# The low part of every weight: a negated copy on ScalarE and an accumulating DMA in place of a subtraction on VectorE

## The chip, the cores and the metric

One core of a Trainium2 chip runs the whole step. The metric is the device time of one execution in microseconds (us). Three timed runs of the kernel before took 2784.03, 2787.16 and 2788.79 us; the median is 2787.16 us.

## The reference

One denoising step of a small backbone with two layers, on 640 tokens of width 1024: 512 latent tokens and 128 context tokens. A layer is a half-step SwiGLU, a token mixer (layer 0: windowed attention; layer 1: a Hyena long convolution) and a second half-step SwiGLU. Each of the six sub-layers is modulated by a condition, gated and normalised.

```python
h = modulate(x, mod[:, 0], mod[:, 1])
f = swiglu(h, ffn_w1, ffn_w2)              # (silu(g) * u) @ w2, with [g, u] = h @ w1 and 2816 hidden columns
x = layer_norm(alpha * x + 0.5 * mod[:, 2] * f)
h = modulate(x, mod[:, 3], mod[:, 4])
out = attn(...)  or  hyena(...)            # projections w_qkv, w_o, or w_in, w_out
x = layer_norm(alpha * x + mod[:, 5] * out)
h = modulate(x, mod[:, 6], mod[:, 7])
x = layer_norm(alpha * x + 0.5 * mod[:, 8] * swiglu(h, ...))
mod = silu(cond) @ ada_w + ada_b           # 9 rows of 1024 a layer
```

All data are float32. The arithmetic is kept near float32 although TensorE multiplies rounded numbers (below).

## The kernel before

**Split operands.** TensorE runs on `float32r`, a rounded float32. So each operand `a` stands as a high part `ah = round(a)` and a low part `al = a - ah`, and a product takes three matmuls: `ah*bh + al*bh + ah*bl`. For weights these are the tiles `wh` and `wl`, for activations `hh`/`hl` (normalised input), `ah`/`al` (SwiGLU), `zh`/`zl` (Hyena).

**Weight units.** All weights come in 170 units in the order of use: tiles of 128 partitions by 2048 numbers (1 MiB), or by 1536 for three quarters of the second SwiGLU matrices (`w2a`, 0.75 MiB). `w_dma` (L108) loads a unit raw from memory into one of two buffers `wr`, by a DMA that SyncE issues. `w_split` (L118) makes the two parts: ScalarE copies `wr` to `wh` with rounding (L93), and VectorE subtracts, `wl = wr - wh` (L94). The subtraction runs on GpSimd in 11 units, which `run_steps` (L520) picks in the groups of three units (six steps), and three more units at the start and in attention are split by other engines (L128, L129). So 167 units go through `split`, the line that is changed. Units are counted from 0 here. After the split the raw buffer is free, and `w_split` asks for the next raw load (L135).

**Order.** Six `w` buffers hold three units. `w_get(u)` (L137) is called at the start of each step on unit u and, where fewer than three are live, splits one unit ahead. As a rule, unit u+2 is split when the first step on u begins, that is, when the matmuls on u-1 have given back their buffers. Engines take their instructions strictly in the order in which the code writes them. The text calls the time from the start of a unit's ScalarE copy to the first matmul that reads its `wl` the slack of the unit.

**Steps.** The 640 tokens run in two halves of 320 columns. A step takes one unit for one half: 48 matmuls of 320 columns. Most units are used for half 0 and at once for half 1; in groups of three units, at the ends of sub-layers, half 0 goes through all three units before half 1, so that the normalisation of half 0 (`ln_sched`, L328) runs beside half 1. It consists of a mean by matmul (`mu`), squares on ScalarE (`sq`), their sum on GpSimd (L351, L354), the reciprocal root on VectorE in small instructions (`rstd`, L470, with `ly` at L475), and a matmul that spreads it (`rs`, L366), for which the next use of `x` waits.

**Beside it.** `bg_step` (L233) computes the modulation in the background: GpSimd issues a 512 KB load `ar` (L231) two steps ahead, VectorE reduces it (L245). A load `ar` waits on GpSimd until VectorE has read the buffer's last contents. Its condition vector `cond` is loaded the same way (L222, 1 MiB).

Of the kernel before, what the change touches and what calls it, by code (L numbers as in the profile page):

```python
# [12 lines left out]
AF = mybir.ActivationFunctionType  # L13
ALU = mybir.AluOpType
# [28 lines left out]
class Kernel:  # L43
# [74 lines left out]
    def w_split(self, copy=None, sub=None):  # L118
        i = self.ws
        if i >= self.wlim:  # L120
            return
        self.w_dma(i + 1)
        shape = self.units[i][1]
        r = self.raw.pop(i)
        hi = self.wp.tile(shape, F32R, tag="w", name="wh")
        lo = self.wp.tile(shape, F32R, tag="w", name="wl")
        if copy is not None:
            copy.tensor_copy(out=hi, in_=r)  # L128
            sub.tensor_tensor(out=lo, in0=r, in1=hi.bitcast(F32), op=ALU.subtract)  # L129
        else:  # L130
            self.split(hi, lo, r, self.weng)
        self.wt[i] = (hi, lo)
        self.wlive.add(i)
        self.ws += 1
        self.w_dma(i + 3)  # L135
# [1631 lines left out]
```

## Time and profile before

| | |
|---|---|
| timed runs, median | 2787.16 us |
| the profiled execution's own time | 2792.72 us |
| its span, first to last instruction | 2791.0 us |
| TensorE (PE) busy | 2697.1 us, 97% |
| VectorE (DVE) busy | 1694.0 us, 61% |
| ScalarE (ACT) busy | 881.7 us, 32% |
| GpSimd (POOL) busy | 579.7 us, 21% |
| moved by DMA | 289.36 MB, mean 104 GB/s |

Busy times are unions of the instructions of an engine. Matmuls overlap each other (each shows some 0.31 us, and they start 0.147 us apart), so PE's busy time says where it had work, not how fast it ran. PEld is the weight load beside the matmuls. SP is SyncE. A DMA's landing is the time at which its data are reported as written.

### The profile page before, as it was taken

To read this page: it belongs to the slowest core of one execution; us is meant where nothing else is said; L and a number is where in the kernel's file an instruction comes from. 1 tells how busy PE (TensorE), PEld (TensorE's weight loads), DVE (VectorE), ACT (ScalarE), POOL (GpSimd) and SP (SyncE) were. 2 spreads that over 40 slices of the span, in tenths; PEclk is the share of its full clock that TensorE was granted. 3 is DMA by queue.
4 is the path that set the end of the run, shared out by engine and by line. 5 is a ranking of instruction groups with operands and counts; after the bars stand their busy time and mean duration, and the time that the engine had idled before them with its cause. 6 is when DMAs were issued, how large, how long until landed. Compare 5 with 4: busy or idle time off the path is not lost. (4 is left out here: it accounts for less than half of the span.)

```text
span 2791.0 us, 42388 instructions
## 1 busy us (share of the span) xinstructions
PE 2697.1 (97%) x17402; PEld 2528.2 (91%) x17402; DVE 1694.0 (61%) x3065; ACT 881.7 (32%) x1507; POOL 579.7 (21%) x639
## 2 busy tenths in 40 slices
PE   9989999998899999999999999999999899999997
PEld 3569999998854999999999999998998899999997
DVE  5865867748965577676766633337658855323334
ACT  3552222214576342222233122224332333122222
POOL 3541000005212520000041000005108842000002
PEclk8889999999899999999999999999999999999998
DMA  6243544421100235454512312221223321212121
GB/s 240 107 158 108 196 154 157 164 83 66 48 3 16 83 111 178 136 181 142 175 68 99 129 62 87 71 85 47 91 90 120 131 80 65 87 61 91 61 76 39
DMA packets 65018, 289.36 MB, mean 104 GB/s; under 512 B 8255, under 2 KB 13583, under 8 KB 46520
## 3 DMA queue, kind: packets, MB, share of 16 engines
q1 hardware_dynamic: 45736, 217.39, 22.4%
q0 software_dynamic: 18720, 69.21, 7.3%
q8 instruction: 137, 2.24, 0.3%
q14 instruction: 57, 0.47, 0.1%
q10 hardware_dynamic: 368, 0.04, 0.0%
HBM read 270.61 MB, written 16.01 MB: 103 GB/s over the span
## 5 line engine op out<-in xcount | busy, mean ns | idle before, releaser
L512 PE MATMUL f<-al,wh 128*128 128x320 f32 (+2 forms) x1408 | 437.3, 311 | 2.1 <-DVE al L94 1.6
L512 PE MATMUL f<-ah,wh 128*128 128x320 f32 (+2 forms) x1408 | 438.1, 311 | 0.0
L553 PE MATMUL g<-hh,wh 128*128 128x320 f32 (+1 forms) x1408 | 437.4, 311 | 0.0
L512 PE MATMUL f<-ah,wl 128*128 128x320 f32 (+2 forms) x1408 | 436.6, 310 | 0.0
L93 ACT ACTIVATE wh<-wr 128x2048 fp32r<-128x2048 f32 (+1 forms) x167 | 297.5, 1783 | 437.3 <-PE f L512 341.2
L553 PE MATMUL g<-hl,wh 128*128 128x320 f32 (+1 forms) x1408 | 435.5, 309 | 0.0
L553 PE MATMUL g<-hh,wl 128*128 128x320 f32 (+1 forms) x1408 | 435.4, 309 | 0.0
L553 PE MATMUL u<-hl,wh 128*128 128x320 f32 (+1 forms) x1408 | 435.3, 309 | 0.0
L553 PE MATMUL u<-hh,wh 128*128 128x320 f32 (+1 forms) x1408 | 435.1, 309 | 0.0
L553 PE MATMUL u<-hh,wl 128*128 128x320 f32 (+1 forms) x1408 | 435.1, 309 | 0.0
L94 DVE TENSOR_TENSOR wl<-wr,wh 128x2048 fp32r<-128x2048 f32 (+1 forms) x156 | 333.4, 2137 | 90.6 <-ACT wh L93 90.2
L563 DVE TENSOR_TENSOR ac<-sg,u 128x320 f32<-128x320 f32 (+1 forms) x176 | 85.8, 487 | 457.7 <-ACT sg L561 457.4
L561 ACT ACTIVATE sg<-g 128x320 f32<-128x320 f32 (+1 forms) x176 | 76.8, 436 | 768.5 <-PE g L553 768.5
L493 DVE SCALAR_TENSOR_TENSOR x<-f,gate,x 128x128 f32<-128x128 f32 (+3 forms) x432 | 172.1, 435 | 204.5 <-PE f L512 204.5
L512 PEld LDWEIGHTS f<-al,wh 128*128 128x128 f32 x1408 | 265.6, 189 | 3.9 <-DVE al L94 3.7
L512 PEld LDWEIGHTS f<-ah,wh 128*128 128x128 f32 x1408 | 265.8, 189 | 1.0 <-ACT ah L93 0.5
L512 PEld LDWEIGHTS f<-ah,wl 128*128 128x128 f32 x1408 | 265.7, 189 | 0.0
L553 PEld LDWEIGHTS g<-hl,wh 128*128 128x128 f32 x1408 | 264.6, 188 | 1.2 <-POOL hl L308 0.5
L553 PEld LDWEIGHTS g<-hh,wh 128*128 128x128 f32 x1408 | 264.5, 188 | 0.8 <-issue 0.3
L553 PEld LDWEIGHTS g<-hh,wl 128*128 128x128 f32 x1408 | 264.4, 188 | 0.1
L553 PEld LDWEIGHTS u<-hh,wl 128*128 128x128 f32 x1408 | 264.4, 188 | 0.0
L553 PEld LDWEIGHTS u<-hh,wh 128*128 128x128 f32 x1408 | 264.4, 188 | 0.0
(300 smaller groups left out, 4837.9 us busy)
## 6 DMA issues: line engine op xcount, KB each, us to landing
wr<-w SPq DMA_DIRECT2D x88, 1024.0 KB
ar<-ada_w POOLq DMA_DIRECT2D x128, 512.0 KB, 3.7
wr<-w2a SPq DMA_DIRECT2D x48, 768.0 KB
wr<-hyin SPq DMA_DIRECT2D x12, 1024.0 KB
wr<-ada_first SPq DMA_DIRECT2D x8, 1024.0 KB
specs<-sg SPq DMA_DIRECT2D x16, 512.0 KB
wr<-w2b SPq DMA_DIRECT2D x8, 1024.0 KB
spec<-specs SPq DMA_DIRECT2D x8, 1024.0 KB
```

Source lines behind the costliest of these rows:

```text
L93: nc.scalar.activation(out=hi, in_=src, func=AF.Copy)
L94: (eng or nc.vector).tensor_tensor(out=lo, in0=src, in1=hi.bitcast(F32), op=ALU.subtract)
L493: nc.vector.scalar_tensor_tensor(out=self.x[:, j, s0:s1], in0=ps[:, s0 - a:s1 - a], scalar=gate[:, tk, j:j + 1], in1=self.x[:, j, s0:s1], ...
L512: nc.tensor.matmul(ps[:, 0:z - a], s[:, kw, c0:c0 + P], m[:, a:z], start=(first and i == 0 and q == 0), stop=(last and i == n - 1 and q == 2))
L553: nc.tensor.matmul(o[:, 0:z - a], s[:, k, c0:c0 + P], m[:, a:z], start=(k == 0 and q == 0), stop=(k == 7 and q == 2))
L561: nc.scalar.activation(out=sg, in_=g[:, 0:z - a], func=AF.Silu)
L563: nc.vector.tensor_tensor(out=ac, in0=sg, in1=uu[:, 0:z - a], op=ALU.mult)
```

## The change

The low part is made another way. ScalarE writes the rounded copy to `wh` as before, and then, in a second instruction of the same size, the negated rounded copy to `wl` (`scale=-1.0`). GpSimd then issues a DMA that reads the unit's raw weights from memory a second time and adds them onto `wl` in place (`accum_op=ALU.add`), so that `wl = -round(w) + w`. VectorE and the 11 GpSimd subtractions are out of it; the choice of engine in `run_steps` has no effect any more. The area for descriptors of GpSimd's DMAs grows from 2048 to 4096 bytes of each partition.

```diff
             copy.tensor_copy(out=hi, in_=r)
             sub.tensor_tensor(out=lo, in0=r, in1=hi.bitcast(F32), op=ALU.subtract)
         else:
-            self.split(hi, lo, r, self.weng)
+            self.nc.scalar.activation(out=hi, in_=r, func=AF.Copy)
+            self.nc.scalar.activation(out=lo, in_=r, func=AF.Copy, scale=-1.0)
+            self.nc.gpsimd.dma_start(out=lo, in_=self.units[i][0], accum_op=ALU.add)
         self.wt[i] = (hi, lo)
...
-    nc = bacc.Bacc("TRN2", target_bir_lowering=False, num_devices=1, dynamic_dma_scratch_size=2048)
+    nc = bacc.Bacc("TRN2", target_bir_lowering=False, num_devices=1, dynamic_dma_scratch_size=4096)
```

Line numbers after the edit are two higher. GpSimd's (POOL's) queue from the first SwiGLU on, before: loads of the modulation (`ar`), one subtraction, sums of a normalisation.

```order
L222 DMA cond<-cB 128x2048
L231 DMA ar<-ada_w 128x1024 x2
L94 TENSOR_TENSOR wl<-wr,wh 128x2048
L231 DMA ar<-ada_w 128x1024 x54
L498 TENSOR_TENSOR sum<-x 128x320
L500 TENSOR_TENSOR sum<-sum,x 128x320 x6
```

The same place with the change:

```order
L224 DMA cond<-cB 128x2048
L233 DMA ar<-ada_w 128x1024 x2
L133 DMA wl<-w 128x2048 x4
L233 DMA ar<-ada_w 128x1024 x2
L133 DMA wl<-w2a 128x1536
L233 DMA ar<-ada_w 128x1024 x2
L133 DMA wl<-w2a 128x1536
L233 DMA ar<-ada_w 128x1024 x4
```

An accumulating DMA of each unit now stands between the loads `ar`, each behind the ScalarE copy that it waits for, and the loads stand behind it.

ScalarE's (ACT's) queue at the end of the Hyena mixer, where its output projection begins, before (`zh` is the projection's input, `sq` the normalisation after it):

```order
L1445 ACTIVATE zh<-yy 128x640 x2
L93 ACTIVATE wh<-wr 128x2048 x3
L346 ACTIVATE sq<-x 128x320 x8
L93 ACTIVATE wh<-wr 128x2048
L300 ACTIVATE h_21502<-x,B,G 128x320
```

and with the change:

```order
L1447 ACTIVATE zh<-yy 128x640 x2
L131 ACTIVATE wh<-wr 128x2048
L132 ACTIVATE wl<-wr 128x2048
L131 ACTIVATE wh<-wr 128x2048
L132 ACTIVATE wl<-wr 128x2048
L131 ACTIVATE wh<-wr 128x2048
L132 ACTIVATE wl<-wr 128x2048
L348 ACTIVATE sq<-x 128x320 x8
```

Each copy is followed by its negated twin, so that the second and third unit's `wh` and the squares come later in this queue.

## Rows read from the trace of the kernel before

**Rows 1.** The page, busy time by engine (us, share of span, instructions).
```profile
PE 2697.1 (97%) x17402; PEld 2528.2 (91%) x17402; DVE 1694.0 (61%) x3065; ACT 881.7 (32%) x1507; POOL 579.7 (21%) x639
```
**Rows 2.** What PE waited for: us in total, times, longest.
```profile
PE rs L366 <- DVE dg L483: 19.1, 8, 4.7
PE v L740 <- DVE sm L774: 3.7, 1, 3.7
```
**Rows 3.** Groups by line: busy us, mean ns, idle before and what ended it.
```profile
L94 DVE TENSOR_TENSOR wl<-wr,wh 128x2048 fp32r<-128x2048 f32 (+1 forms) x156 | 333.4, 2137 | 90.6 <-ACT wh L93 90.2 <-issue 0.3
L94 POOL TENSOR_TENSOR wl<-wr,wh 128x2048 fp32r<-128x2048 f32 x11 | 51.6, 4694 | 48.3 <-ACT wh L93 48.1
L93 ACT ACTIVATE wh<-wr 128x2048 fp32r<-128x2048 f32 (+1 forms) x167 | 297.5, 1783 | 437.3 <-PE f L512 341.2 <-issue 96.0
L231 POOL DMA_DIRECT2D ar<-ada_w x128 | 67.8, 530 | 737.6 <-DVE mods L245 692.7 <-DVE x L493 21.6 <-DVE gate L280 16.5
```
**Rows 4.** DMA queue of GpSimd; its issues: KB each, us to landing.
```profile
q0 software_dynamic: 18720, 69.21, 7.3%
ar<-ada_w POOLq DMA_DIRECT2D x128, 512.0 KB, 3.7
cond<-cB POOLq DMA_DIRECT2D x2, 1024.0 KB, 6.0
```
**Rows 5.** Timeline (start us, us), unit 64 of `w2a`: copy, and first matmul on `wl`.
```profile
1183.26 1.47 ACT L93 ACTIVATE wh<-wr 128x1536 fp32r<-128x1536 f32 x1
1203.48 0.31 PE L512 MATMUL f<-ah,wl 128*128 128x320 f32 x1
```
**Rows 6.** Timeline, units 2, 39, 41, 130, 131: copy, and first matmul on `wl`.
```profile
195.43 1.90 ACT L93 ACTIVATE wh<-wr 128x2048 fp32r<-128x2048 f32 x1
199.70 0.42 PE L553 MATMUL g<-hh,wl 128*128 128x320 f32 x1
701.19 1.92 ACT L93 ACTIVATE wh<-wr 128x2048 fp32r<-128x2048 f32 x1
709.21 0.31 PE L512 MATMUL k<-hh,wl 128*128 128x320 f32 x1
739.22 1.91 ACT L93 ACTIVATE wh<-wr 128x2048 fp32r<-128x2048 f32 x1
744.82 0.58 PE L740 MATMUL v<-wl,hh 128*128 128x256 f32 x1 [3.25 <-DVE wl L94]
2218.42 1.90 ACT L93 ACTIVATE wh<-wr 128x2048 fp32r<-128x2048 f32 x1
2223.10 0.41 PE L512 MATMUL f<-zh,wl 128*128 128x320 f32 x1
2240.51 1.90 ACT L93 ACTIVATE wh<-wr 128x2048 fp32r<-128x2048 f32 x1
2246.16 0.31 PE L512 MATMUL f<-zh,wl 128*128 128x320 f32 x1
```
**Rows 7.** Timeline, unit 3, split inside the first group of three: the same.
```profile
214.78 1.90 ACT L93 ACTIVATE wh<-wr 128x2048 fp32r<-128x2048 f32 x1
227.96 0.31 PE L553 MATMUL g<-hh,wl 128*128 128x320 f32 x1
```
**Rows 8.** VectorE at L475: group by form; ns min/median/max; one instance on the timeline.
```profile
L475 DVE TENSOR_SCALAR ly<-lv 80x4 int32<-80x4 int32 x10 | 15.6, 1555 | 0.3
L475 DVE TENSOR_SCALAR ly<-lv x12: 161/167/3992, 642.2 to 2778.4; 80x4 int32<-80x4 int32 x10, 96x4 int32<-96x4 int32 x1, 64x4 int32<-64x4 int32 x1
1426.39 4.59 POOL L94 TENSOR_TENSOR wl<-wr,wh 128x2048 fp32r<-128x2048 f32 x1
1427.45 3.55 DVE L475 TENSOR_SCALAR ly<-lv 80x4 int32<-80x4 int32 x1
```
**Rows 9.** Windows: busy us and count by engine, PEclk, DMA share, GB/s.
```profile
1015.00:1400.00 385.00, 385.00 (x2627) 385.00 (x2626) 276.45 (x430) 86.10 (x104) 31.79 (x60) 1.00 0.47 158
```

## The prediction, made before the changed kernel ran

> **What bounds the kernel now.** I read the page's busy row first [rows 1]: PE has work for 2697.1 of 2791.0 us, VectorE for 1694.0. So the end is set by matmuls, and taking work off VectorE pays only where PE waits for VectorE. The view of PE's waits says where that is: the largest entry is 19.1 us over 8 waits of `rs`, the spread of the reciprocal root in a normalisation [rows 2]. All of PE's idle time is 2791.0 - 2697.1 = 94 us, and a good part lies in the first 185 us, before the first weight unit. No wait for a weight's low part is among the large ones, although 156 subtractions take 333.4 us of VectorE [rows 3]: they are hidden. The timeline of single units shows by what. In the plain run of the SwiGLU the copy of unit 64 starts at 1183.26 and its `wl` is first read at 1203.48, a slack of 20.2 us [rows 5]; the row stands for the 142 of the 167 units that have 16 us or more. At the other end are five units whose slack is 199.70 - 195.43 = 4.3, 8.0, 5.6, 4.7 and 5.7 us (units 2, 39, 41, 130, 131) [rows 6]; 20 more lie between 9.9 and 15.2, most of them like unit 3 with 13.2 [rows 7], the units of the groups of three and those split inside them.
>
> **The change part by part.**
>
> *Removed.* 333.4 us of VectorE and 51.6 us of GpSimd in 11 subtractions of 4.69 us [rows 3]. Hidden by PE's queue, hence nothing by themselves, with one exception. At 1426.39 GpSimd subtracts for 4.59 us, and the small VectorE instruction at L475 that starts at 1427.45 lasts 3.55 us, to the moment the subtraction ends [rows 8]; its median is 0.167 us. It is the first of the reciprocal root's steps, for which `rs` waits. Ten of them take 15.6 us where ten undisturbed ones take 1.7: 13.9 us that PE waits for [rows 2, 8]. With the subtraction on GpSimd gone I credit 14 us.
>
> *Added on ScalarE.* A second instruction of the same size on each of 167 units, 297.5 us more [rows 3], to some 1180 us. ScalarE has the time, but the copy is now followed by 1.9 us in its own queue, and `wl` isn't begun on another engine.
>
> *Added on GpSimd.* 167 issues; a load `ar` costs 0.53 us to issue [rows 3], one with twice the reads I put at 0.65. That is 109 us on GpSimd against 52 saved. Each waits in GpSimd's queue for ScalarE's second copy, with sums and loads `ar` behind it. The subtraction it replaces waited there for the first copy and then ran 4.69 us, so what is behind is let go no later than before in the normalisations; in the SwiGLU only the `ar` loads are behind, which are needed two steps later.
>
> *Added on the DMA engines.* 167 accumulating transfers, 162 MB. The trace has none, so I bound the landing by the plain ones. GpSimd's queue moved 69.21 MB in 7.3% of 16 engines' 2791 us, that is 3260 engine-us, 49.4 for 1 MiB or 3.09 us on all 16. Half of that from the 3.7 us of a 512 KB load leaves 2.16 us fixed [rows 4]. A plain 1 MiB would land after 5.25 us (the row of `cond`, with other loads behind it, says 6.0). That is the lower end. The add has to read its target too: with two passes 2.16 + 2 x 3.09 = 8.3 us; with read, read and write in turn 11.4 us. No row excludes an add that is slower still; I put the upper end at 16 us, five passes and a little. Further, the raw load of the unit after next starts when ScalarE is through with `wr`, so exactly beside the add, and takes up to 3.09 us of the same engines: 8.3 to 11.4 again. I take 9.6 us, near the two-pass row with part of that load beside it.
>
> The Trainium skill bears on this price. "Collectives: The Full Stack", section "The bandwidth ceiling: the fold count and why AG ≠ RS ≠ AR", says that a reducing transfer runs at half the rate of a copy because it takes two source reads, not because the add costs time; "DMA: Bandwidth & Descriptors", section "Anatomy of one DMA — SWDGE (gpsimd) path", puts a DMA at about 2.0 us and bytes at 436 GB/s. Together they estimate 6.8 us for 1 MiB, and by the sum below some 30 us of stalls in place of 60. Against the copy it speaks as my bound does; no run here shows an add so far.
>
> *The path.* From the copy's start to a usable `wl` it is now 1.9 + 1.9 + 0.65 + 9.6 = 14.05 us, where copy and subtraction took about 4.2 [rows 3]. The steady units hold it: unit 64 needs 1.48 + 1.48 + 0.65 and, at three quarters of the size, 7.7 us = 11.3 of its 20.2 [rows 5]. The five tight units don't: 14.05 less their slack is 9.8 + 6.0 + 8.4 + 9.4 + 8.4 = 42 us of PE standing still, since PE's queue can't go round a missing operand. The 20 next ones lose little each: going through them in order, each stall moving all that follows, I get 4 us at unit 43 (slack 9.9), 3.5 at unit 133 (10.6), and 10.5 at 13 others (unit 3: 14.05 - 13.2 = 0.9), 18 in all. Total 60. Of it 4 us are covered, since the value matmuls that read unit 41 wait 3.7 us for VectorE anyway soon after [rows 2], and the 14 of the normalisation come back. 60 - 4 - 14 = +42 us.
>
> *Whether the DMA engines hold it.* From 1015 to 1400 us, with raw weights and modulation loads, they are busy 0.47 of the time [rows 9]. PE takes 1 MiB in 14.1 us (96 matmuls at 0.147 us), 27.3 MiB in these 385 us; at two passes of 3.09 us that adds 169 us or 0.44, 0.91 in all. They hold it, barely, so landings in this stretch will be late, inside a slack of 20.
>
> The profiled execution took 2792.72 us, 5.6 more than the median of the timed runs; I keep that distance. 2792.7 + 42 = 2834.7 in its terms and **2829 us** in the median's.
>
> **The rivals.**
>
> *The add is much slower, and the DMA engines become the bound.* For it: 0.91 leaves no room. At three passes the same stretch needs 0.47 + 0.66 = 1.13. Modulation is loaded during about 825 us, so 0.13 x 825 = 107 us, and with 11.4 us of landing the tight units lose 99 instead of 60. 107 + 99 - 18 = +188, 2975 us; a middle course, late landings without saturation, about +110. Against it: nothing in the trace, as it has no add. It decides from about 2.2 passes on.
>
> *Stalls and relief cancel.* With the plain copy's 5.25 us the path is 9.7 us; the five lose 5 x 9.7 - 28.2 = 20 us, the others nearly nothing. 20 - 4 - 14 = +2, 2789 us. For it: engines may read and write at once, so that the second read costs little. Against: the doubled read goes through the same queue.
>
> *Faster.* The mechanism is the normalisation's wait, and it is more than L475: VectorE without 2.3 us subtractions reaches every step of the chain before `rs` sooner, so that all eight waits go, 19.1 us, and 3.7 at the value matmuls [rows 2]. With a landing of 4.4 us, less than any 1 MiB load here, the five lose 5 x 8.85 - 28.2 = 16. 16 - 22.8 = -7, 2780 us. It decides below about 4.7 us. Against it: `cond`'s 6.0 us [rows 4] without any add.
>
> **How the numbers follow.** A measurement of this kernel tells a change of 0.2%, 5.6 us, from none. Forecast, +15 to +80 us: 0.50. Slow add, above +80: 0.20. Cancelled, within 5.6: 0.15. Faster: 0.10. The remaining 0.05 are small losses of 6 to 15 us. Slower is thus 0.50 + 0.20 + 0.05 = 0.75, same 0.15, faster 0.10. The likeliest case alone spans 2802 to 2867 us. The range for eight in ten takes in the cancelled case and half of the slow one: 2783 to 2930 us.
>
> **What would show it.** VectorE's busy time falls to about 1360 us, ScalarE's rises to about 1180, GpSimd's to about 635; the queue q0 carries some 230 MB. The issues of `wl` list a landing: 8 to 11 us confirms the price, below 5.5 or above 12 makes one of the rivals. PE's waits name the DMA of `wl` with some 60 us, most of it at units 2, 39, 41, 130 and 131, and none at a unit in the middle of a SwiGLU; stalls spread over those, with DMA shares above 0.95 from 230 to 600 and 1015 to 1400 us, mean the slow add. L475 at 0.17 us throughout and `rs` waits down to about 5 us confirm the credit. If PE waits little for `wl` and the time is still longer, the fault is elsewhere: in sums that stand on GpSimd behind an issue, or in squares behind ScalarE's second copy.

## The result and the profile after

The changed kernel takes 2852.57 us in the median of 4 runs (2850.81 to 2856.26); the kernel before took 2787.97 us in the 4 runs beside it (2784.03 to 2791.06). The ratio is 1.0229, with a 95% interval of 1.0212 to 1.0245: slower by some 64 us. The forecast was 2829 us with a range of 2783 to 2930. The profiled execution took 2856.26 us, 63.5 more than that of before.

Busy time by engine on the page, which answers to [rows 1]:

```profile
PE 2712.1 (95%) x17402; PEld 2541.8 (89%) x17402; DVE 1341.4 (47%) x2909; ACT 1160.3 (41%) x1674; POOL 652.7 (23%) x795
```

VectorE lost 353 us, ScalarE gained 279 and GpSimd 73, and the end came later all the same. PE's work is the same 17402 matmuls, but its busy time grew by 15 us: some of them ran slower, which a wait alone does not do.

The groups behind it, for [rows 3] (busy us, mean ns of one, idle before and what ended it):

```profile
L132 ACT ACTIVATE wl<-wr 128x2048 fp32r<-128x2048 f32 (+1 forms) x167 | 296.3, 1774 | 0.0
L133 POOL DMA_DIRECT2D wl<-w x86 | 76.5, 889 | 499.6 <-ACT wl L132 497.6 <-issue 1.6
```

The negated copy costs what the first one costs, 1.77 us. GpSimd's issue of an add takes 0.89 us, not 0.65.

The DMA queues and the landings (KB each, median us from issue to landing), for [rows 4]:

```profile
q0 software_dynamic: 42768, 231.75, 35.9%
wl<-w POOLq DMA_DIRECT2D x86, 1024.0 KB, 11.0
ar<-ada_w POOLq DMA_DIRECT2D x128, 512.0 KB, 6.7
wl<-hyout POOLq DMA_DIRECT2D x4, 1024.0 KB, 14.2
wl<-wo POOLq DMA_DIRECT2D x3, 1024.0 KB, 16.5
```

An add of 1 MiB lands after 11.0 us in the median, counted from the start of its issue, where 9.6 had been put; two groups that are issued close together take 14 to 17. The modulation loads went from 3.7 to 6.7 us.

PE's waits (us in total, times, longest), for [rows 2]:

```profile
PE g L555 <- DMA wl<-w: 28.9, 9, 11.8
PE f L514 <- DMA wl<-hyout: 22.3, 2, 12.1
PE k L514 <- DMA wl<-wqkv: 6.7, 1, 6.7
PE f L514 <- DMA wl<-wo: 5.9, 1, 5.9
PE v L742 <- DMA wl<-wqkv: 4.8, 1, 4.8
PE vp L362 <- DVE sq L356: 4.7, 1, 4.7
PE f L514 <- DMA wl<-w2b: 3.9, 3, 1.9
PE f L514 <- DMA wl<-w2a: 3.3, 1, 3.3
PE u L514 <- DMA wl<-hyin: 3.1, 2, 2.1
PE rs L368 <- DVE dg L485: 1.2, 2, 0.8
PE mu L340 <- POOL sum L502: 0.8, 2, 0.4
```

This view names the cause and its counterweight. The eight rows with a DMA of `wl` sum to 78.9 us over 20 waits; before there was none. `rs` fell from 19.1 us to 1.2, and `mu` from 4.6 to 0.8. The value matmuls (`v`), which waited 12.3 us for VectorE and ScalarE before, now wait 4.8 for an add.

The windows around two of the long stalls show what lies behind them (start:end, length, busy us and count of PE, PEld, DVE, ACT and POOL, then the granted clock, the DMA share and GB/s):

```profile
200.00:211.70 11.70, 0.00 (x0) 0.00 (x0) 1.50 (x4) 1.26 (x3) 0.48 (x1) 0.62 0.96 281
211.70:216.00 4.30, 4.25 (x16) 4.25 (x17) 0.00 (x0) 0.00 (x0) 0.00 (x0) 0.50 0.01 4
216.00:222.00 6.00, 6.00 (x41) 6.00 (x40) 0.49 (x1) 0.91 (x2) 0.00 (x0) 0.96 0.00 0
...
2256.90:2269.00 12.10, 0.05 (x1) 0.05 (x1) 5.98 (x7) 2.01 (x5) 3.41 (x4) 0.67 0.96 283
2269.00:2275.00 6.00, 6.00 (x23) 6.00 (x24) 0.00 (x0) 0.00 (x0) 0.00 (x0) 0.53 0.00 2
...
1015.00:1400.00 385.00, 383.68 (x2616) 383.41 (x2615) 214.28 (x397) 143.22 (x150) 63.53 (x95) 1.00 0.81 224
```

PE stands still for 11.7 us, and then nothing holds it back but its clock: 16 matmuls in 4.30 us at a granted clock of 0.50, the 1.2 GHz level, where the next 6.00 us at 0.96 hold 41. At 2269 it is 23 in 6.00 us at 0.53. The last row, beside [rows 9], is the modulation stretch: a DMA share of 0.81, and a clock of 1.00.

Both traces hold the 17402 matmuls in the same order, so the distances from each matmul's start to the next one's can be paired. Where a distance differs by over 0.3 us, the longer ones of after add 84.5 us (78.9 of `wl` and the new wait `vp`, 4.7) and the shorter ones take off 35.0. The many small differences add 14.1 us: 16.2 in the 20 us behind each of the nine distances that grew by over 2.5 us, and -2.1 everywhere else. 84.5 - 35.0 + 14.1 = 63.6 us, all of the loss.

### The profile page after: what moved, and what is told of

Read it like the earlier page. It is cut to its first block, busy times and chain, and to the rows that moved or that the text cites. A ratio compares the mean times of both kernels' runs of the same rounds, so it can differ in the third digit from the quotient of the medians.

```text
span 2854.4 us, 42699 instructions
## 1 busy us (share of the span) xinstructions
PE 2712.1 (95%) x17402; PEld 2541.8 (89%) x17402; DVE 1341.4 (47%) x2909; ACT 1160.3 (41%) x1674; POOL 652.7 (23%) x795
## 3 DMA queue, kind: packets, MB, share of 16 engines
q0 software_dynamic: 42768, 231.75, 35.9%
## 5 line engine op out<-in xcount | busy, mean ns | idle before, releaser
L132 ACT ACTIVATE wl<-wr 128x2048 fp32r<-128x2048 f32 (+1 forms) x167 | 296.3, 1774 | 0.0
L555 PEld LDWEIGHTS u<-hl,wh 128*128 128x128 f32 x1408 | 266.2, 189 | 0.0
```

The lines of the kernel that those rows point to most:

```text
L132: self.nc.scalar.activation(out=lo, in_=r, func=AF.Copy, scale=-1.0)
L555: nc.tensor.matmul(o[:, 0:z - a], s[:, k, c0:c0 + P], m[:, a:z], start=(k == 0 and q == 0), stop=(k == 7 and q == 2))
```

## The experiments

Each expectation sets an account of the stalls, of the landing or of the credit, called theory A, against others. The account as a whole is: the stalls at units with little slack make the loss, and the freed small instruction of the normalisation makes the credit. The first four ran beside a kernel before of 2786.6 us (median of 15 runs, 2782.69 to 2794.66), the last four beside 2786.94 us (7 runs, 2785.71 to 2789.62).

**Only the units with room keep the DMA.** 28 units whose slack is under 17 us are split by ScalarE and VectorE as before.

```diff
+            if i in TIGHT:
+                self.split(hi, lo, r)
+            else:
                 ... copy, negated copy, accumulating DMA
```

> The 28 units with less than 17 us of slack before are split as before (ScalarE copy, VectorE subtraction); the other 139 keep the accumulating DMA. Theory A (the loss is PE standing at tight units, plus TensorE's low clock after long stalls): no wait of PE for a DMA of wl is left, the clock drops behind the stalls go, and the credit at the normalisations (rs and mu waits, 16 to 20 us) stays: 2765 to 2780 us. Theory B (the doubled DMA traffic and the longer ScalarE and GpSimd queues slow the kernel everywhere, stalls being only where it shows): most of the traffic is still there, so most of the loss too: above 2825 us.

Measured: 2778.34 us (9 runs, 2768.09 to 2782.3), ratio 0.9961, 0.9948 to 0.9975. The only wait of PE for an add:

```profile
PE f L519 <- DMA wl<-w2a: 2.8, 1, 2.8
```

139 adds still run, with 202.39 MB in GpSimd's DMA queue and a landing of 11.1 us. Without the tight units the rest costs PE 2.8 us in one place, and theory A's 2765 to 2780 us is met. So the loss is in the stalls. What the traffic of 139 adds and ScalarE's second copy cost by themselves is a few us at most: the version with only five adds (below) is 6.1 us faster, and the two intervals overlap.

**A plain copy in place of the add.** The DMA overwrites `wl`; the addition is left out.

```diff
-            self.nc.gpsimd.dma_start(out=lo, in_=self.units[i][0], accum_op=ALU.add)
+            self.nc.gpsimd.dma_start(out=lo, in_=self.units[i][0])
```

> The DMA of each unit overwrites wl with the raw weight in place of adding to it; the low parts are therefore whole weights, the addition is left out. Waits, queues and bytes from memory stay the same. Theory A (the landing of 11.0 us is fixed 2.2 + two passes of 3.1 + some 2.7 for the raw load that runs beside it): one pass less, landings of about 5.3 us alone and 8 beside a raw load, PE's waits for wl fall from 79 to about 45 us, time about 2808 us. Theory B (the landing is long because the transfer starts late behind GpSimd's queue and the raw load, and not for the add): landings stay at 10 to 11 us and the time at 2850 us.

Measured: 2790.19 us, a single run. The queue and the landing of most units:

```profile
q0 software_dynamic: 42768, 231.75, 22.0%
wl<-w POOLq DMA_DIRECT2D x86, 1024.0 KB, 7.5
```

and the two largest of PE's waits for `wl`:

```profile
PE f L514 <- DMA wl<-hyout: 15.7, 2, 10.6
PE g L555 <- DMA wl<-w: 11.9, 3, 8.0
```

The same bytes take 22.0% of the DMA engines instead of 35.9%. Take off the 7.3% of the modulation loads [rows 4], and the 155 MiB of the weights cost 0.147 x 16 x 2788.3 / 155 = 42.3 engine-us a MiB as a copy and 0.286 x 16 x 2854.4 / 155 = 84.3 as an add, 2.65 and 5.27 us on all 16 engines: twice. The Trainium skill, "Collectives: The Full Stack", section "The bandwidth ceiling: the fold count and why AG ≠ RS ≠ AR", says of collectives that a ReduceScatter runs at half an AllGather's rate, a reduce against a copy, because of its second read. The doubling agrees with that; that the read and not the addition is the cause, no run here shows. The copy's 7.5 us is longer than the 5.25 of the plain bound, because a raw load runs beside it: the one of unit 39, beside none, lands after 5.1. Even the copy stalls PE for 27.6 us in these two rows and for 36.7 in all. Theory A was right on the landing (about 8 beside a raw load), but its time was 18 us too long: the waits fell by 42 us where it had 34, and the small differences between paired matmuls by 19.

**The credit alone.** The kernel before, with the add at only five units (36, 46, 82, 118, 134), those whose GpSimd subtraction falls on the reciprocal root.

```diff
+            if i in ADDED:
+                ... copy, negated copy, accumulating DMA
+            else:
                 self.split(hi, lo, r, self.weng)
```

> The kernel before, except that units 36, 46, 82, 118 and 134, whose GpSimd subtraction runs into the reciprocal root of a normalisation, get the ScalarE twin and the accumulating DMA. Theory A (what the change won is the collision at L475 alone): the rs waits fall from 19 to about 3 us, mu waits by 2 more, nothing stalls since these units have 17 us or more of slack: 2769 to 2775 us. Theory B (the credit came from VectorE being free of 156 subtractions): these five leave VectorE as it is, so 2783 to 2790 us.

Measured: 2772.24 us (6 runs, 2768.0 to 2778.15), ratio 0.9947, 0.9931 to 0.9963: 14.4 us faster than before. The first step of the reciprocal root (ns min/median/max, first and last start):

```profile
L482 DVE TENSOR_SCALAR ly<-lv x12: 161/166/1203, 636.5 to 2756.3; 80x4 int32<-80x4 int32 x10, 96x4 int32<-96x4 int32 x1, 64x4 int32<-64x4 int32 x1
```

and PE's waits around it:

```profile
PE rs L373 <- DVE dg L490: 3.5, 5, 1.9
PE mu L345 <- POOL sum L507: 8.9, 6, 2.6
```

The longest of the twelve instructions went from 3992 ns [rows 8] to 1203, `rs` from 19.1 us to 3.5, and 4.3 us of that came back at `mu`. The two traces thus show 11.3 us, and the medians 14.4 with an interval of some 10 to 19. That is a credit of about 14 us without any stall, and the lowest median of all versions. Not all of it is L475: four of the five subtractions fell on that instruction, and the fifth on the next one, L476, which takes 0.17 us undisturbed. In the kernel before:

```profile
2279.64 4.56 POOL L94 TENSOR_TENSOR wl<-wr,wh 128x2048 fp32r<-128x2048 f32 x1
2279.74 4.48 DVE L476 TENSOR_SCALAR ly<-ly 80x4 int32<-80x4 int32 x1
```

**The same collision removed without a DMA.** The kernel before, with its 11 GpSimd subtractions given to VectorE.

```diff
-            self.split(hi, lo, r, self.weng)
+            self.split(hi, lo, r)
```

> The kernel before with the 11 GpSimd subtractions given to VectorE, no accumulating DMA at all. Theory A: the collision at L475 goes, but 2.3 us of subtraction now stand on VectorE ahead of the reciprocal root, where 3.4 stood before: rs waits fall only by a few us, 2778 to 2787 us. Theory B (any subtraction near the normalisation costs the same wherever it runs): no change, 2785 to 2791 us.

Measured: 2775.14 us (7 runs, 2773.05 to 2782.73), ratio 0.9964, 0.9949 to 0.998. The same instruction here:

```profile
L475 DVE TENSOR_SCALAR ly<-lv x12: 161/166/781, 645.0 to 2767.0; 80x4 int32<-80x4 int32 x10, 96x4 int32<-96x4 int32 x1, 64x4 int32<-64x4 int32 x1
```

and PE's wait behind it:

```profile
PE rs L366 <- DVE dg L483: 7.0, 6, 1.9
```

Three us below what was expected, and not told apart from the version with five adds: the intervals overlap. What helps is that GpSimd doesn't subtract then. The DMA isn't needed for it.

**Raw loads behind the adds.** The changed kernel, with the raw loads issued by GpSimd.

```diff
-            nc.sync.dma_start(out=r, in_=src)
+            nc.gpsimd.dma_start(out=r, in_=src)
```

> The changed kernel, with the raw loads of the weight units issued by GpSimd instead of SyncE, so that they stand behind the accumulating DMA in the same queue. Theory A (the add lands after 11.0 us because the raw load issued beside it goes first; alone it takes 8.2 to 8.4): landings fall to 8.3 to 8.6 us, each of the 20-odd stalls loses up to 2.7 us, together about 40 of the 79 us, and with the clock's share the time is 2805 to 2813 us. Rival 1 (an engine shares its time between the two transfers in whatever queue they stand): landings stay at 10.5 to 11.5 us and the time at 2850 to 2857. Rival 2 (raw loads now come late, since they stand in GpSimd's queue behind the second copy, and become the new wait): PE or ScalarE wait for the DMA of wr, 2860 us or more.

Measured: 2803.94 us (4 runs, 2802.22 to 2807.7), ratio to before 1.006, 1.0045 to 1.0075. Landing of most units:

```profile
wl<-w POOLq DMA_DIRECT2D x86, 1024.0 KB, 8.9
```

and one of the two largest waits of PE for `wl`, with unit 2 as its longest:

```profile
PE g L555 <- DMA wl<-w: 13.2, 3, 9.4
```

Landings fall to 8.9 us and, for other matrices, down to 8.0, and the waits for `wl` from 78.9 to 44.8. One line of code gives back 48.6 us of the 64.6: 34.1 us of waits, and 13.4 of the small differences behind them. The time is 1 us below theory A's range, and the landing somewhat above its 8.3 to 8.6. The changed kernel's own trace bears it out in two single adds with no other transfer in GpSimd's queue, issued at 1626.97 beside a raw load and at 2775.64 beside none. The first line below is all that the two queues moved from 1626.9 to 1630.9 us, the others are the two landings:

```profile
q1 hardware_dynamic: 120, 0.98, 86.8%
wl<-w POOLq DMA_DIRECT2D x1, 1024.0 KB, 10.8
wl<-w2b POOLq DMA_DIRECT2D x1, 1024.0 KB, 8.3
```

For its first 4 us the add moves nothing, while 0.98 of the load's 1.05 MB goes by in SyncE's queue (q1). 8.3 us is the two-pass row of the prediction. By the estimate from the Trainium skill's two pages it would have been 6.8; the measurement decides.

The second longest stall has another cause besides. Ahead of unit 2's add stand `cond` and two loads `ar`, 2 MiB, in GpSimd's own queue of the changed kernel:

```profile
195.73 0.74 POOL L224 DMA_DIRECT2D cond<-cB  x1
196.46 1.07 POOL L233 DMA_DIRECT2D ar<-ada_w  x2
199.58 0.90 POOL L133 DMA_DIRECT2D wl<-w  x1 [2.04 <-ACT wl L132]
```

This add lands after 12.1 us. With the raw loads behind it, it still takes 10.2, and PE still waits 9.4.

**The three longest stalls removed.** The changed kernel with units 2, 130 and 131 split on VectorE, in the form of the first experiment.

```diff
+TIGHT = {2, 130, 131}
```

> The changed kernel, but units 2, 130 and 131, which cause the three longest stalls (11.8 + 12.1 + 10.2 = 34.1 us), are split by ScalarE and VectorE as before the change. Theory A (stall plus a granted clock of half speed behind a long stall; small steps behind these three add up to 2.2 + 4.85 = 7 us): 40 to 42 us less than the changed kernel, 2811 to 2813, and the granted clock just behind 200 and 2290 us is back near 1.00. Rival (the stalls alone; the low clock would have come anyway): 34 us less, 2818 or 2819, and the clock rows stay near 0.5 to 0.6. Rival 2 (the following units inherit the stall): less than 25 us, above 2827.

Measured: 2813.69 us (4 runs, 2811.56 to 2819.82), 38.9 less than the changed kernel; ratio to before 1.0091, 1.0074 to 1.0108. The windows of the first stall, as shown of the changed kernel:

```profile
200.00:211.70 11.70, 11.70 (x81) 11.70 (x81) 5.64 (x14) 2.18 (x5) 0.00 (x0) 1.00 0.45 185
211.70:216.00 4.30, 4.30 (x32) 4.30 (x31) 0.98 (x2) 2.02 (x3) 0.00 (x0) 1.00 0.00 0
```

and the wait that is left at `hyout`:

```profile
PE f L519 <- DMA wl<-hyout: 5.9, 1, 5.9
```

Where there is no stall, the clock stays at 1.00, and 4.30 us hold 32 matmuls instead of 16: the low clock is the stall's doing. The unit after the two of `hyout` now waits 5.9 us itself, so 34.1 - 5.9 = 28 us of stalls went. The two profiled executions differ by 36.4 us: 28.3 in the distances that grew, 9.8 in the small differences, and -1.7 in the rest. Theory A's time is missed by less than 1 us, but the shares are other than its 34 and 7. Behind the three stalls themselves the small differences had added 2.1 + 2.4 + 2.5 = 7 us over before; the rest of the 9.8 lies where the two kernels do the same, and its cause is open.

**All five tight units.** As before, with units 39 and 41 as well.

```diff
+TIGHT = {2, 39, 41, 130, 131}
```

> The changed kernel, but the five tight units of the prediction (2, 39, 41, 130, 131) are split by ScalarE and VectorE as before the change. Their five stalls sum to 11.8 + 6.7 + 4.8 + 12.1 + 10.2 = 45.6 us. Theory A (each unit pays for itself, with about 8 us for the clock): 2797 to 2802 us, and the 25 to 33 us of stalls at other units stay. Rival (units 42, 43 and others inherit the stall of 39 and 41): nearer to the kernel with three units than 5 us.

Measured: 2820.43 us (4 runs, 2814.19 to 2826.31), ratio to before 1.0118, 1.01 to 1.0135: no better than with three, and theory A's 2797 to 2802 is missed. PE's waits at the value matmuls:

```profile
PE v L747 <- DVE sm L781: 5.0, 1, 5.0
PE v L747 <- DVE wl L96: 3.3, 1, 3.3
PE v L747 <- ACT qs L633: 1.6, 1, 1.6
PE v L747 <- ACT wh L95: 0.5, 1, 0.5
```

With three units PE waited here for the adds of units 39 and 41, 6.6 + 4.0 = 10.6 us; with five it waits 10.4 us there for VectorE and ScalarE, 6.6 for the attention's own work and 3.8 for the split of the unit. The kernel before waited 12.3 us in the same four places. So taking these two stalls away gives nothing back. Why the median is nominally higher by 6.7 us is open: the profiled execution with five is 5.6 us shorter than that with three, the runs of both scatter over 8 to 12 us, and the two intervals overlap.

**The add reads the chip's own raw buffer.**

```diff
-            self.nc.gpsimd.dma_start(out=lo, in_=self.units[i][0], accum_op=ALU.add)
+            self.nc.gpsimd.dma_start(out=lo, in_=r, accum_op=ALU.add)
```

> The changed kernel, but the accumulating DMA reads the raw weights from the raw buffer on the chip (wr) instead of from memory a second time. Theory A (the price of an add is its two passes over the engines, 8.3 us, plus the raw load that starts beside it): the raw buffer is now free only after the add has landed, so no raw load starts beside it; landings of 8.3 to 9 us, stalls of some 40 us, 2805 to 2815 us. Rival 1 (the second read from memory is what costs, and a read on the chip is cheap): landings of 5 to 6 us, 2785 to 2795. Rival 2 (raw buffers come free 8 us late and the copies then wait for raw loads): as long as the changed kernel or longer, with ScalarE waiting for the DMA of wr.

Measured: 2832.0 us (4 runs, 2829.37 to 2837.13), ratio to before 1.0162, 1.0146 to 1.0177. The waits of PE, VectorE and SyncE that tell it:

```profile
PE vp L362 <- DVE sq L356: 17.7, 2, 15.6
DVE sinkn L665 <- DMA sinkn<-sinkb: 16.1, 1, 16.1
SPq L114 <- DMA wl<-wr: 2149.2, 162, 50.3
```

and the landings:

```profile
wl<-wr POOLq DMA_DIRECT2D x119, 1024.0 KB, 8.2
```

This median mixes adds in different company. One with nothing beside it lands sooner (610.3 to 617.5 us; so do most of the 41 such adds of 1 MiB, median 7.0):

```profile
wl<-wr POOLq DMA_DIRECT2D x1, 1024.0 KB, 7.0
```

From memory the three that stand alone in the changed kernel take 8.3 to 9.0. So a source on the chip lands at least 1.3 us sooner, although the adds take the same time of the DMA engines (36.0% of 2832.4 us here, 35.9% of 2854.4 in the changed kernel). That is not the first rival's 5 to 6 us, and its 2785 to 2795 us is missed by far. Theory A is missed by 17 us too: PE's waits for `wl` still sum to 55.0 us, where it had some 40, and a raw load can fall beside an add here as well (10.3 us for the add at 735.37). The wait that the second rival named does appear, though the kernel is 20.6 us faster than the changed one:

```profile
ACT wh L131 <- DMA wr<-w: 170.2, 22, 16.0
```

SyncE now holds each raw load until the add has landed, and the attention's small loads stand behind it: `sinkn` comes 16 us late to VectorE, the normalisation's sum of squares is behind that, and PE waits 15.6 us. A queue that waits passes the wait on to what stands behind it.

## Why the prediction was right, and where its sum was off

The sign and the mechanism held: PE can't go round a late `wl`, stalls appear at the units with little slack, and the normalisation gives a part back. The traffic is held (0.81 in the stretch from 1015 to 1400 us, against 0.91 worked out with 6.18 us of the engines a MiB, where an add takes 5.27), so the slow add as a bound fell, and with 11.0 us the cancelling and the faster case too. Of the signs, the landing came out at the very edge of its 8 to 11 us, and L475's longest instance fell from 3.99 us to 1.19, not to 0.17. The sum was +42; in the traces it is +63.6. The difference by terms:

- **The landing, 9.6 us: mis-sized, 11.0 measured.** The pass was nearly right (8.3 to 9.0 alone). The step that failed is "up to 3.09 us of the same engines", of which less than half was taken; nearly the whole load goes first. In the steady stretches a raw load is issued beside each add. A small error goes the other way: a landing is counted from the start of the issue, so the 0.65 us for the issue was in it already. From a unit's copy to its add's issue 4.0 us pass, and the path is 4.0 + 11.0 = 15.0 us against 14.05.
- **The stalls, 60 us: 78.9 measured.** The five tight units were 11.8 + 6.7 + 4.8 + 12.1 + 10.2 = 45.6 against 42; unit 41 lost 3.6 us less, the others 0.7 to 2.7 more, unit 2 because of the loads ahead of it in its queue. The others were 33.3 over 15 waits against 18: each path is 1.0 us longer, and one steady unit (3.3 us at `w2a`) was not forecast at all.
- **The credit, 14 + 4: 35.0 measured.** `rs` gave 18.5 us of it. The 14 us for L475 are borne out, but the sum left out the fifth collision, 4.3 us at L476. The experiment with five adds removes this collision too and gives 4.3 us back at `mu`, so its 14.4 us meets the forecast 14 by luck. `mu` gave 4.4 us here. 10 us are value matmuls, which only wait elsewhere now; that relief was put at 4 us. The rest, 2.4 us, is scattered.
- **A term that the sum lacked: 14.1 us of small differences,** nearly all of it behind stalls; where windows were read there, TensorE ran at half its clock (0.50 and 0.53). A stall was priced at its own length.

+18.9 (stalls) - 17.0 (credit) + 14.1 (small differences) + 5.6 (`vp` and the rest of the longer distances) = +21.6, which is 63.6 - 42. The 2829 us was thus nearer than its terms deserved, and that is luck: stalls and a relief that were both put too small, by about the same amount, cancel. Two readings were wrong without bearing on the sum: 16 us of landing is four and a half passes, not five and a little, and only 17 of PE's 94 us of idle time lie in the first 185 us.

## What to carry to other kernels

Work that is hidden by a queue's slack is worth nothing to remove, and a slower substitute costs its excess at each place where the slack is shorter than its latency: list the slack unit by unit before choosing, and change only the units that can bear it, or only those that gain (here five units of 167 gave 14.4 us, the same gain came without any DMA, and the change as a whole lost 64). Price a DMA with what stands beside and ahead of it in all queues, and a stall of TensorE with the slow matmuls behind it. Before adding up stalls, ask which of them another engine would cause anyway.

## What was not expected of the hardware

- After PE had stood still for 11.7 us the granted clock was 0.50 for the next 4.30 us (16 matmuls instead of 32); the three longest stalls together cost some 7 us beyond themselves.
- An accumulating DMA occupies the DMA engines for 5.27 us a MiB, a copy of the same bytes for 2.65. With nothing beside it, 1 MiB lands after 8.3 to 9.0 us from memory and after 7.0 from the chip's own buffer.
- A raw load that SyncE issues at the same time lands ahead of GpSimd's add: 11.0 us for the add beside it, 8.0 to 8.9 where the same load stands behind it in GpSimd's queue.
